# A two-layer trunk on one core: the state-space mixer's drive in two row tiles, its table fetched once, and u and y sent from other queues

## The chip, the cores and the metric

One core of a Trainium2 chip runs the whole program in one launch. The metric is device time in microseconds (us), less is better. The engines are TensorE (PE, with its weight loads shown apart as PEld), VectorE (DVE), ScalarE (ACT), GpSimd (POOL) and SyncE (SP); each takes its instructions in the order of its own queue. SP, ACT and POOL can issue DMAs; the profile shows them as SPq, ACTq and POOLq.

## The reference

The input is 256 tokens by 2048 features in float32, the depth two. Each layer is a mixer and then a gated feed-forward network with a causal convolution, both with a residual add. Layer 0 has a spatial-gating mixer; layer 1, which the change concerns, has a state-space mixer:

```python
u = h @ w_in                                     # 128 groups of 16 channels
bu = einsum('gpc,btgc->btgp', bbar, u)           # complex, 64 states per group
h_t = abar * h_{t-1} + bu_t                      # a complex diagonal recurrence over tokens
y = einsum('gcp,btgp->btgc', c_re, h.re) - einsum('gcp,btgp->btgc', c_im, h.im) + d * u
ga, gb = split(gelu(y) @ w_glu)
out = ga * sigmoid(gb)
```

## The kernel before

All large products are made on TensorE in 32-bit pieces. A weight tile (up to 1 MB, `tag="raw"`, three buffers) is fetched by SP (L108), split into units of 128x1024: ACT rounds a unit to `wh` (L124), DVE subtracts to get the rest `wl` (L125); five buffers of each. Each product then takes three matmuls, `wh` by X, `wl` by X and `wh` by X's rest (L786 and L787 in one layout, L893 to L895 in the other).

Layer 0 and its feed-forward network fill the time to about 1046 us. Then the state-space mixer follows. Its input product runs in 8 groups of two weight tiles (`form_a`, accumulators `acc`); each group gives u for two blocks of 128 features (s = 0 to 15 in all). A block s of u is then worked on in steps that the class `S5Tokens` holds, and a program of slots (one slot for each weight tile, `N_OF`, `at`, `step`) says which step of which block is traced after which tile. With n the slot of `drive`:

- `send` (L543): u goes from the tile `u` (two buffers) to DRAM (`ud`), right behind the group that made it.
- `load` (slot n-1): u comes back from DRAM in another layout, two DMAs (L551), as block-diagonal `ubd` (four buffers, off-diagonal zeros), and the matrix `pw` (L556). `load1`: the table of cosines and sines `tab` (three buffers) comes twice, to partitions 0 to 63 and again to 64 to 127 (L566). `load2` (slot n+1): `qw` and `tw` (L574, L576).
- `drive` (slot n): four matmuls of 128 rows by 128 columns of weights, `pw` by `ubd`, into the PSUM tile `ps_x` (L584).
- `take`, `scan` (n+1), `turn` (n+2): ACT copies and negates halves of `ps_x` (L597, L598), DVE multiplies by the table and adds (L599 to L609), runs the recurrence (L610) and multiplies by the table again (L623 to L625).
- `outputs` (n+3): matmuls from `ubd` with `tw` and from `sp` with `qw`, each into one half of the partitions (L639, L645).
- `gelu` (n+4): ACT makes `y`; two DMAs take it to DRAM (`yd`, L655). `fetch` (n+4): POOL brings it back as `yt` (L661). `finish` (n+6): ACT and DVE split `yt` into the operand `Gt` (L1168, L1169).

The second product (`w_glu`, tiles of `group_b` with accumulators `accb`) begins behind the eighth group, first over the blocks s = 0 to 7, and the last slots run beside it. SP's queue holds, in one order, the weights, u out and in, `pw`, `tab`, `qw`, `tw` and y; POOL's holds only `fetch`. The order of each engine's queue isn't the order of the source: the framework lays it out beforehand from simulated times and from the data dependences, and puts in the waits.

PSUM has 8 banks: three accumulators of two banks each (`acc_ps`), and two banks (`misc_ps`) that `ps_x`, `ps_y` and all small tiles share.

Of the kernel before, what the change touches and what calls it, by code (L numbers as in the profile page):

```python
# [9 lines left out]
F32 = mybir.dt.float32  # L10
# [3 lines left out]
ALU = mybir.AluOpType  # L14
PSUM = bass.MemoryType.PSUM
DRAM = bass.MemoryType.DRAM

P = 128
# [13 lines left out]
def dram(ap, offset, dims):  # L32
    return bass.AP(ap.tensor, ap.offset + offset, dims)
# [20 lines left out]
def rsqrt_column(nc, v, y, t, w):  # L54

    V = nc.vector
    V.tensor_scalar(y.bitcast(I32), v.bitcast(I32), -0.5, RSQ, ALU.mult, ALU.add)
    V.tensor_scalar(w, v, -0.5, None, ALU.mult)
    for _ in range(3):
        V.scalar_tensor_tensor(t, y, w, y, ALU.mult, ALU.mult)  # L60
        V.scalar_tensor_tensor(y, t, 1.5, y, ALU.add, ALU.mult)
# [13 lines left out]
class Weights:  # L75


    def __init__(self, nc, pool, tiles):
        self.nc, self.pool, self.tiles = nc, pool, tiles
        self.raw, self.halves = {}, {}  # L80
        self.n_dma = self.n_split = self.n_get = 0
        self.units = []
        for i, (segs, nk, width) in enumerate(tiles):
            for o in range(0, nk * width, 1024):
                self.units.append((i, o, min(1024, nk * width - o)))
        self.first_unit = {}
        for u, (i, o, n) in enumerate(self.units):
            self.first_unit.setdefault(i, u)
# [428 lines left out]
class S5Tokens:  # L517


    def __init__(self, tc, pool, psum, scr, rho, emit):  # L520
        self.nc, self.pool, self.psum = tc.nc, pool, psum
        self.scr, self.rho, self.emit = scr, rho, emit
        self.u, self.st = {}, {}
        self.ubd, self.sp = [], []
        for i in range(4):
            t = pool.tile([P, 4, P], F32, name=f"ubd{i}", tag=f"ubd{i}")
            self.nc.gpsimd.memset(t, 0.0)
            self.ubd.append(t)
        for i in range(2):
            t = pool.tile([P, 8, 64], F32, name=f"sp{i}", tag=f"sp{i}")  # L530
            self.nc.gpsimd.memset(t, 0.0)
            self.sp.append(t)
        self.rt = pool.tile([P, 8, 64], F32, name="rt")
        self.nc.gpsimd.memset(self.rt, 0.0)
# [5 lines left out]
    def send(self, s):  # L540

        ud = self.scr[4]
        self.nc.sync.dma_start(dram(ud, s * 32768, [[256, P], [1, 256]]), self.u.pop(s).rearrange("p j k -> p (j k)"))  # L543

    def load(self, s):

        nc, pool = self.nc, self.pool
        pd, qd, td, rd, ud, yd = self.scr
        ubd = self.ubd[s % 4]
        for h2 in range(2):  # L550
            nc.sync.dma_start(  # L551
                ubd[64 * h2 : 64 * h2 + 64, :, 64 * h2 : 64 * h2 + 64],
                dram(ud, s * 32768 + h2 * 4096, [[64, 64], [8192, 4], [1, 64]]),
            )
        pw = pool.tile([P, 4, P], F32, name=f"pw{s}", tag="pw", bufs=2)
        nc.sync.dma_start(pw, dram(pd, s * 65536, [[128, P], [16384, 4], [1, 128]]))  # L556
        self.st[s] = dict(pw=pw, ubd=ubd)

    def load1(self, s):

        rd = self.scr[3]
        tab = self.pool.tile([P, 2, 512], F32, name=f"tab{s}", tag="tab", bufs=3)
        lh = 8 * s % 64
        o = ((lh // 16) * P + 64 * (s // 8)) * 2048 + (lh % 16) * 64
        for i in range(2):
            self.nc.sync.dma_start(tab[64 * i : 64 * i + 64], dram(rd, o, [[2048, 64], [1024, 2], [1, 512]]))  # L566
        self.st[s]["tab"] = tab

    def load2(self, s):
# [9 lines left out]
    def drive(self, s):  # L579

        st = self.st[s]
        st["x"] = self.psum.tile([P, 512], F32, name=f"ps_x{s}", tag="misc")
        for i in range(4):
            self.nc.tensor.matmul(  # L584
                st["x"][:, i * P : (i + 1) * P], st["pw"][:, i, :], st["ubd"][:, i, :], start=True, stop=True
            )

    def take(self, s):

        nc, pool = self.nc, self.pool  # L590
        V, A = nc.vector, nc.scalar
        st = self.st[s]
        ps = st["x"]
        q = pool.tile([P, 512], F32, name=f"q{s}", tag="q", bufs=2)
        x = pool.tile([P, 512], F32, name=f"x{s}", tag="x", bufs=2)
        cos, sin = st["tab"][:, 0, :], st["tab"][:, 1, :]
        A.copy(x[0:64], ps[64:128])  # L597
        A.mul(x[64:128], ps[0:64], -1.0)  # L598
        V.tensor_tensor(q, ps, cos, op=ALU.mult)  # L599
        V.tensor_tensor(x, x, sin, op=ALU.mult)  # L600
        st["q"], st["dx"] = q, x

# [47 lines left out]
    def gelu(self, s):  # L650
        st = self.st.pop(s)
        y = self.pool.tile([P, 4, 64], F32, name=f"y{s}", tag="y", bufs=2)
        self.nc.scalar.activation(y.rearrange("q h k -> q (h k)"), st["y"][:, :256], AF.Gelu_apprx_tanh)
        for i in range(2):
            self.nc.sync.dma_start(  # L655
                dram(self.scr[5], s * 32768 + i * 16384, [[64, 64], [4096, 4], [1, 64]]), y[64 * i : 64 * i + 64]
            )

# [10 lines left out]
def tile_hybrid_trunk(  # L669
# [6 lines left out]
    nc = tc.nc  # L676
    V, A, T, G = nc.vector, nc.scalar, nc.tensor, nc.gpsimd
# [2 lines left out]
    const = ctx.enter_context(tc.tile_pool(name="const", bufs=1))  # L680
    dpool = ctx.enter_context(tc.tile_pool(name="scratch", bufs=1, space=DRAM))
    wpool = ctx.enter_context(tc.tile_pool(name="weights", bufs=1))
    acc_ps = ctx.enter_context(tc.tile_pool(name="acc_ps", bufs=3, space=PSUM))
    misc_ps = ctx.enter_context(tc.tile_pool(name="misc_ps", bufs=2, space=PSUM))


    def ffn_groups(l):
# [52 lines left out]
    rho = const.tile([P, NH], F32, name="rho")  # L740
# [6 lines left out]
    scr = []  # L747
# [86 lines left out]
    def square_sum(tp, src, dst):  # L834
        tag, bufs = tmp[0]
        junk = tp.tile([P, 512], F32, name="junk", tag=tag, bufs=bufs)
        return A.activation(junk[:, : src.shape[-1]], src, AF.Square, accum_out=dst)
# [170 lines left out]
    with ExitStack() as sgu_ctx:  # L1008
        sp = sgu_ctx.enter_context(tc.tile_pool(name="sgu", bufs=1))
# [69 lines left out]
        for g in range(4):  # L1079
            st = {}  # L1080
# [77 lines left out]


    tmp[0] = ("t", 1)  # L1160
    with tc.tile_pool(name="s5", bufs=1) as sp:

        Ys = [None] * KC

# [4 lines left out]
            V.tensor_tensor(lo, yv, hi.bitcast(F32), op=ALU.subtract)  # L1169
            Ys[s] = g  # L1170

        s5 = S5Tokens(tc, sp, misc_ps, scr, rho, emit)
        rbv = rbc.rearrange("p (k j) -> p j k", j=4)
        sched = {}

# [87 lines left out]


    tmp[0] = ("a", 2)
    with tc.tile_pool(name="ffn1", bufs=1) as fpool:
        fg = fpool.tile([P, D], F32, name="fg")
        nc.gpsimd.dma_start(fg, dram(final_g, 0, [[0, P], [1, D]]))
        oss = fpool.tile([P, 2, 4], F32, name="oss")
        tails = [[fpool.tile([P, 1], F32, name=f"o{n}{a}") for n in "svrtw"] for a in range(2)]  # L1270
        os_ = out2.rearrange("(a p) d -> p a d", p=P)

        def fin(g, pss, toks):
            cs = slice(512 * g, 512 * g + 512)
            for a in toks:
                V.tensor_tensor(hn[:, a, cs], hn[:, a, cs], pss[a], op=ALU.add)
            for a in toks:
                square_sum(fpool, hn[:, a, cs], oss[:, a, g : g + 1])
                if g < 3:
                    V.tensor_tensor(hn[:, a, cs], hn[:, a, cs], fg[:, cs], op=ALU.mult)  # L1280
                s, v, r, t, w = tails[a]
                if g == 2:
                    V.tensor_tensor(s, oss[:, a, 0:1], oss[:, a, 1:2], op=ALU.add)
                    V.tensor_tensor(s, s, oss[:, a, 2:3], op=ALU.add)
                    V.tensor_scalar(s, s, 1.0 / D, EPS, ALU.mult, ALU.add)
                if g == 3:
                    V.scalar_tensor_tensor(v, oss[:, a, 3:4], 1.0 / D, s, ALU.mult, ALU.add)
                    rsqrt_column(nc, v, r, t, w)
                    for q in range(4):
                        hq = hn[:, a, 512 * q : 512 * q + 512]  # L1290
                        if q == 3:
                            V.scalar_tensor_tensor(hq, hq, r, fg[:, cs], ALU.mult, ALU.mult)
                        elif q:
                            A.mul(hq, hq, r)
                        else:
                            V.tensor_scalar(hq, hq, r, None, ALU.mult)
                        nc.sync.dma_start(os_[:, a, 512 * q : 512 * q + 512], hq)

        ffn(1, None, fin)
# [32 lines left out]
```

## Time and profile before

| | |
|---|---|
| median of 3 runs | 2120.24 us (2118.4 to 2120.79) |
| the profiled execution | 2121.23 us, its span 2119.5 us |
| PE busy | 2090.7 us, 99% of the span |
| DVE, ACT, POOL busy | 68%, 54%, 4% |
| moved by DMA | 438.59 MB, 207 GB/s in the mean |

The span is the time from the first to the last instruction in one profiled execution; some 1.7 us of the execution lie outside it. A busy PE means that matmuls are in flight. "PEclk" is the granted share of TensorE's clock: 1 is 2.4 GHz, a half is 1.2 GHz.

### The profile page before, as it was taken

The page shows a single profiled execution, that of the slowest core. Times are in us where ns is not written, and L with a number is a line of the kernel's source. Part 1 is how long each engine was busy: PE and PEld are TensorE (multiplying, and loading weights), DVE is VectorE, ACT ScalarE, POOL GpSimd, SP SyncE. Part 2 cuts the span into 40 slices and gives each one's busy share as a digit, 9 for nine tenths or more (in the row PEclk, how much of TensorE's full clock was granted, in tenths as well). Part 3 has the DMA queues.
Part 4 walks back from the last instruction along what each step waited for, and adds up shares of the span by engine and source line. Part 5 has one row for each costly group of instructions (what it writes and reads, how often), then busy time and mean ns, then how long its engine had stood idle before and what let it go on. Part 6 is the DMA issues. An engine that isn't in the chain of part 4 may idle for free.

```text
span 2119.5 us, 27328 instructions
## 1 busy us (share of the span) xinstructions
PE 2090.7 (99%) x10279; PEld 1736.8 (82%) x10279; DVE 1439.0 (68%) x2123; ACT 1134.6 (54%) x1656; POOL 90.3 (4%) x142
## 2 busy tenths in 40 slices
PE   9999999999999999999998999999999999999998
PEld 7888888888888788888887788888888888888886
DVE  5476777886896645888788766766555656546665
ACT  6544456554555544555556556655544555445553
POOL 1010000000111110000000000000000000000000
PEclk9999999999999999999999999999999999999999
DMA  8655556666777666565799986565556555565553
GB/s 279 201 180 179 187 192 199 212 236 225 217 241 238 214 213 191 184 223 202 233 263 260 273 269 206 179 211 185 172 194 201 188 182 187 190 197 181 193 183 120
DMA packets 358597, 438.59 MB, mean 207 GB/s; under 512 B 31712, under 2 KB 275520, under 8 KB 357824
## 3 DMA queue, kind: packets, MB, share of 16 engines
q1 hardware_dynamic: 349008, 407.94, 60.5%
q0 software_dynamic: 9424, 28.88, 4.6%
q8 instruction: 81, 1.33, 0.3%
q14 instruction: 52, 0.43, 0.1%
q10 hardware_dynamic: 32, 0.01, 0.0%
HBM read 414.66 MB, written 22.02 MB: 206 GB/s over the span
## 4 chain that ended last, share of the span: by engine, by line
PE 95%; DMA 3%; DVE 1%; ACT 0%; SPq 0%; issue 0%; ACTq 0%; DVEq 0%; POOLq 0%
PE accb L893 26%; PE accb L894 26%; PE accb L895 26%; PE acc L786 4%; PE acc L787 2%; PE zt L916 2%; PE accv L987 1%; PE accv L988 1%; PE accv L989 1%; DMA w<-in_b_w_glu_dram 1%; PE pt L821 1%; DMA w<-in_b_w_in_dram 1%; DMA tab<-rd 1%; DMA ubd<-ud 0%; PE ps_x L584 0%; DMA ud<-u 0%
## 5 line engine op out<-in xcount | busy, mean ns | idle before, releaser
L125 DVE TENSOR_TENSOR wl<-w,wh 128x1024 fp32r<-128x1024 f32 (+1 forms) x721 | 879.4, 1222 | 581.2 <-ACT wh L124 577.9
L124 ACT CAST wh<-w 128x1024 fp32r<-128x1024 f32 (+1 forms) x721 | 754.1, 1050 | 744.5 <-PE accb L895 608.5
L895 PE MATMUL accb<-wh,X 128*128 128x512 f32 x1408 | 552.8, 393 | 0.0
L893 PE MATMUL accb<-wh,X 128*128 128x512 f32 x1408 | 552.1, 392 | 0.0
L894 PE MATMUL accb<-wl,X 128*128 128x512 f32 x1408 | 549.5, 390 | 0.0
L893 PE MATMUL accb<-wh,Gt 128*128 128x512 f32 x1060 | 415.8, 392 | 0.0
L895 PE MATMUL accb<-wh,Gt 128*128 128x512 f32 x1060 | 414.3, 391 | 0.0
L894 PE MATMUL accb<-wl,Gt 128*128 128x512 f32 x1060 | 414.2, 391 | 0.0
L895 PEld LDWEIGHTS accb<-wh,X 128*128 128x128 f32 x1408 | 264.4, 188 | 56.8
L894 PEld LDWEIGHTS accb<-wl,X 128*128 128x128 f32 x1408 | 264.6, 188 | 54.5
L893 PEld LDWEIGHTS accb<-wh,X 128*128 128x128 f32 x1408 | 264.5, 188 | 53.7
L893 PEld LDWEIGHTS accb<-wh,Gt 128*128 128x128 f32 x1060 | 199.2, 188 | 41.6
L895 PEld LDWEIGHTS accb<-wh,Gt 128*128 128x128 f32 x1060 | 199.2, 188 | 41.5 <-issue 0.2
L894 PEld LDWEIGHTS accb<-wl,Gt 128*128 128x128 f32 x1060 | 199.3, 188 | 41.1 <-issue 0.2
L786 PE MATMUL acc<-X,wh 128*128 128x512 f32 x512 | 184.0, 402 | 0.0
L787 PE MATMUL acc<-X,wl 128*128 128x256 f32 x512 | 144.8, 283 | 0.0
L786 PEld LDWEIGHTS acc<-X,wh 128*128 128x128 f32 x512 | 97.2, 190 | 21.8
L924 ACT ACTIVATE a<-zt,conv 128x256 f32<-128x256 f32 x176 | 94.2, 557 | 14.3 <-PE zt L916 8.2
L787 PEld LDWEIGHTS acc<-X,wl 128*128 128x128 f32 x512 | 97.9, 191 | 0.2
L943 ACT ACTIVATE z<-accb,rtok 128x512 f32<-128x512 f32 x88 | 55.7, 684 | 66.5 <-PE accb L895 66.5
L925 DVE SCALAR_TENSOR_TENSOR a<-zt,conv,a 128x255 f32<-128x255 f32 x176 | 77.7, 476 | 13.0 <-ACT a L924 13.0
L928 DVE SCALAR_TENSOR_TENSOR a<-zt,conv,a 128x254 f32<-128x254 f32 x176 | 77.1, 474 | 0.7
(299 smaller groups left out, 1407.3 us busy)
## 6 DMA issues: line engine op xcount, KB each, us to landing
w<-in_f_w_up_dram SPq DMA_DIRECT2D x352, 512.0 KB, 4.6
w<-in_f_w_down_dram SPq DMA_DIRECT2D x80, 1024.0 KB, 5.2
w<-in_b_w_glu_dram SPq DMA_DIRECT2D x64, 512.0 KB, 5.1
w<-in_a_w_in_dram SPq DMA_DIRECT2D x28, 1024.0 KB, 5.3
w<-in_a_w_out_dram SPq DMA_DIRECT2D x16, 1024.0 KB, 5.1
w<-in_b_w_in_dram SPq DMA_DIRECT2D x16, 1024.0 KB, 7.9
w<-in_f_w_down_dram SPq DMA_DIRECT2D x16, 512.0 KB, 3.7
tab<-rd SPq DMA_DIRECT2D x32, 256.0 KB, 6.7
```

The costliest lines, as they stand in the source:

```text
L124: self.nc.scalar.copy(hi[:, a:b], raw[:, o + a : o + b])
L125: self.nc.vector.tensor_tensor(lo[:, a:b], raw[:, o + a : o + b], hi[:, a:b].bitcast(F32), op=ALU.subtract)
L786: T.matmul(ps, wh, Xt[k], start=k == k_first, stop=False, skip_group_check=True)
L787: T.matmul(ps[:, NT:], wl, Xt[k][:, :NT], start=False, stop=k == ktot - 1, skip_group_check=True)
L893: T.matmul(ps[:, tt, :], xh, wh, start=k == k_first, stop=False)
L894: T.matmul(ps[:, tt, :], xh, wl, start=False, stop=False)
L895: T.matmul(ps[:, tt, :], xl, wh, start=False, stop=k == ktot - 1)
L916: T.transpose(pt[:, v * NT + tt * P : v * NT + (tt + 1) * P], z[:, tt, v * NT + q * P : v * NT + (q + 1) * P], ident,)
L924: A.activation(a[:, v], zt, AF.Identity, bias=cw[:, 3, cv : cv + 1], scale=cw[:, 2, cv : cv + 1])
L925: V.scalar_tensor_tensor(a[:, v, 1:], zt[:, : NT - 1], cw[:, 1, cv : cv + 1], a[:, v, 1:], ALU.mult, ALU.add)
L928: V.scalar_tensor_tensor(a[:, v, 2:], zt[:, : NT - 2], cw[:, 0, cv : cv + 1], a[:, v, 2:], ALU.mult, ALU.add)
L943: A.mul(z[:, tt], ps[:, tt], rtok[:, tt : tt + 1])
```

## The change

`drive` makes eight matmuls with 64 rows and 64 columns of moving data each, where it made four with 128 and 128. Since `ubd` is block-diagonal, the two halves of the rows give different columns, and each half goes to a row tile of its own (`tile_position`) and a PSUM bank of its own. `ps_x` has two banks for that and a pool of its own with one buffer; within the mixer the accumulators have two buffers, not three, and the pools of accumulators are closed and opened again before and behind it. `take` reads `ps_x` in the new order. The table is fetched once, to partitions 0 to 63, and ACT copies it to the others. `send` and the two `ubd` loads are issued by POOL, the two DMAs of y by ACT.

```diff
-        self.nc.sync.dma_start(dram(ud, ...), self.u.pop(s)...)
+        self.nc.gpsimd.dma_start(dram(ud, ...), self.u.pop(s)...)
...
         for h2 in range(2):
-            nc.sync.dma_start(
+            nc.gpsimd.dma_start(
                 ubd[64 * h2 : 64 * h2 + 64, :, 64 * h2 : 64 * h2 + 64],
...
-        for i in range(2):
-            self.nc.sync.dma_start(tab[64 * i : 64 * i + 64], dram(rd, o, [[2048, 64], [1024, 2], [1, 512]]))
+        self.nc.sync.dma_start(tab[:64], dram(rd, o, [[2048, 64], [1024, 2], [1, 512]]))
+        self.nc.scalar.copy(tab[64:], tab[:64])
...
-        st["x"] = self.psum.tile([P, 512], F32, name=f"ps_x{s}", tag="misc")
+        xt = self.xps.tile([P, 2, 512], F32, name=f"ps_x{s}", tag="x")[:, :, :256]
         for i in range(4):
-            self.nc.tensor.matmul(
-                st["x"][:, i * P : (i + 1) * P], st["pw"][:, i, :], st["ubd"][:, i, :], start=True, stop=True
-            )
+            for b in range(2):
+                o = 64 * b
+                self.nc.tensor.matmul(
+                    xt[:, b, i * 64 : i * 64 + 64], st["pw"][o : o + 64, i, :], st["ubd"][o : o + 64, i, o : o + 64],
+                    start=True, stop=True, tile_position=(o, 0),
+                )
+        st["x"] = xt.rearrange("p b (i k) -> p i b k", k=64)
...
-        A.copy(x[0:64], ps[64:128])
-        A.mul(x[64:128], ps[0:64], -1.0)
-        V.tensor_tensor(q, ps, cos, op=ALU.mult)
+        x4, q4, c4 = (t.rearrange("p (i b k) -> p i b k", i=4, b=2) for t in (x, q, cos))
+        A.copy(x4[0:64], ps[64:128])
+        A.mul(x4[64:128], ps[0:64], -1.0)
+        V.tensor_tensor(q4, ps, c4, op=ALU.mult)
...
-            self.nc.sync.dma_start(
+            self.nc.scalar.dma_start(
                 dram(self.scr[5], s * 32768 + i * 16384, [[64, 64], [4096, 4], [1, 64]]), y[64 * i : 64 * i + 64]
...
+    acc_ctx.close()
+    with ExitStack() as s5_ctx:
+        acc_ps = s5_ctx.enter_context(tc.tile_pool(name="acc_s5", bufs=2, space=PSUM))
+        xps = s5_ctx.enter_context(tc.tile_pool(name="x_ps", bufs=1, space=PSUM))
...
+        acc_ps = ffn_ctx.enter_context(tc.tile_pool(name="acc_f1", bufs=3, space=PSUM))
```

## Rows read from the trace of the kernel before

**Rows 1.** Page, part 1: PE's busy time, share, instructions
```profile
PE 2090.7 (99%) x10279; PEld 1736.8 (82%) x10279; DVE 1439.0 (68%) x2123; ACT 1134.6 (54%) x1656; POOL 90.3 (4%) x142
```
**Rows 2.** Waits of PE, 1050 to 1330 us: total, times, longest
```profile
PE ps_x L584 <- DMA ubd<-ud: 12.9, 4, 7.2
PE ps_x L584 <- DVE q L609: 1.1, 1, 1.1
```
**Rows 3.** Timeline of PE: start us, us, [idle before <-releaser]
```profile
1131.13 2.04 PE L584 MATMUL ps_x<-ubd,pw 128*128 128x128 f32 x8 [7.20 <-DMA ubd<-ud]
...
1139.51 0.66 PE L639 MATMUL ps_y<-ubd,tw 128*64 128x128 f32 x8
...
1140.81 1.13 PE L584 MATMUL ps_x<-ubd,pw 128*128 128x128 f32 x8 [0.17 <-DMA tab<-rd]
...
1147.52 0.66 PE L639 MATMUL ps_y<-ubd,tw 128*64 128x128 f32 x8
...
1186.52 2.05 PE L584 MATMUL ps_x<-ubd,pw 128*128 128x128 f32 x8 [3.37 <-DMA ubd<-ud]
```
**Rows 4.** Chain that ended last, 1100 to 1260 us: start us, us, what
```profile
1193.81 0.59 PE ps_y L639 x8
...
1212.41 0.89 PE ps_x L584 x8
1218.75 0.59 PE ps_y L639 x8
1219.34 0.47 PE ps_y L645 x16
```
**Rows 5.** Busy time of each engine by stretch; last PEclk, DMA share, GB/s
```profile
1125.00:1150.00 25.00, 17.64 (x131) 15.42 (x132) 20.16 (x29) 13.16 (x20) 1.07 (x2) 0.86 1.00 251
...
1075.00:1200.00 125.00, 110.46 (x794) 93.69 (x794) 105.48 (x138) 76.31 (x112) 6.25 (x11) 0.95 0.99 262
1059.00:1200.00 141.00, 126.46 (x888) 107.88 (x887) 114.98 (x148) 84.43 (x122) 6.25 (x11) 0.95 0.99 264
```
**Rows 6.** Timeline of SP: the two loads of ubd for s = 6
```profile
1119.23 1.25 SPq L551 DMA_DIRECT2D ubd<-ud  x2
```
**Rows 7.** DMA landing times: of ubd<-ud (by SP), then of yt<-yd (by POOL)
```profile
DMA to landing us min/median/max: 2.3/5.5/11.3
...
DMA to landing us min/median/max: 2.6/5.2/6.4
```
**Rows 8.** DMA issues, 1040 to 1330 us: count, KB each, median us to landing
```profile
q1 hardware_dynamic: 81525, 70.27, 86.2%
...
tab<-rd SPq DMA_DIRECT2D x32, 256.0 KB, 6.7
...
ubd<-ud SPq DMA_DIRECT2D x32, 64.0 KB, 5.5
yd<-y SPq DMA_DIRECT2D x32, 64.0 KB, 6.5
```
**Rows 9.** Issue durations by line: ns min/median/max, first and last start us
```profile
L655 SPq DMA_DIRECT2D yd<-y x32: 581/608/1771, 1101.7 to 1266.2; - x32
...
L661 POOL DMA_DIRECT2D yt<-yd x16: 536/537/556, 1108.6 to 1270.7; - x16
...
L471 POOL DMA_DIRECT2D td<-tt x16: 1491/1498/1557, 641.4 to 846.1; - x16
```
**Rows 10.** Groups of ACT, 1059 to 1200 us: busy, mean ns, idle before
```profile
L124 ACT CAST wh<-w 128x1024 fp32r<-128x1024 f32 x35 | 36.8, 1050 | 39.0 <-PE acc L786 21.2 <-DMA w<-in_b_w_glu_dram 11.1 <-DMA w<-in_b_w_in_dram 6.5
```
**Rows 11.** Weight loads of two lines: ns min/median/max
```profile
L584 PEld LDWEIGHTS ps_x<-ubd,pw x128: 185/192/334, 1078.2 to 1239.0; 128*128 128x128 f32 x128
...
L645 PEld LDWEIGHTS ps_y<-sp,qw x256: 132/138/139, 1097.0 to 1257.8; 128*64 128x64 f32 x128
```
**Rows 12.** Timeline of DVE: the last residual ahead of the mixer
```profile
1046.20 1.23 DVE L860 TENSOR_TENSOR hn<-accb,hn 128x1024 f32<-128x1024 f32 x1 [0.35 <-PE accb L895]
```

More of the change, by code (lines that the diff above doesn't have):

```diff
@@ L517, with __init__ @@
 class S5Tokens:
-    def __init__(self, tc, pool, psum, scr, rho, emit):
-        self.nc, self.pool, self.psum = tc.nc, pool, psum
+    def __init__(self, tc, pool, psum, xps, scr, rho, emit):
+        self.nc, self.pool, self.psum, self.xps = tc.nc, pool, psum, xps
         self.scr, self.rho, self.emit = scr, rho, emit
@@ L542, in send @@
         ud = self.scr[4]
-        self.nc.sync.dma_start(dram(ud, s * 32768, [[256, P], [1, 256]]), self.u.pop(s).rearrange("p j k -> p (j k)"))
+        self.nc.gpsimd.dma_start(dram(ud, s * 32768, [[256, P], [1, 256]]), self.u.pop(s).rearrange("p j k -> p (j k)"))
     def load(self, s):
@@ L682, in tile_hybrid_trunk @@
     wpool = ctx.enter_context(tc.tile_pool(name="weights", bufs=1))
-    acc_ps = ctx.enter_context(tc.tile_pool(name="acc_ps", bufs=3, space=PSUM))
     misc_ps = ctx.enter_context(tc.tile_pool(name="misc_ps", bufs=2, space=PSUM))
+    acc_ctx = ExitStack()
+    acc_ps = acc_ctx.enter_context(tc.tile_pool(name="acc_ps", bufs=3, space=PSUM))
     def ffn_groups(l):
@@ L1160, in tile_hybrid_trunk @@
     tmp[0] = ("t", 1)
-    with tc.tile_pool(name="s5", bufs=1) as sp:
+    acc_ctx.close()
+    with ExitStack() as s5_ctx:
+        acc_ps = s5_ctx.enter_context(tc.tile_pool(name="acc_s5", bufs=2, space=PSUM))
+        xps = s5_ctx.enter_context(tc.tile_pool(name="x_ps", bufs=1, space=PSUM))
+        sp = s5_ctx.enter_context(tc.tile_pool(name="s5", bufs=1))
         Ys = [None] * KC
@@ L1170, in emit @@
             Ys[s] = g
-        s5 = S5Tokens(tc, sp, misc_ps, scr, rho, emit)
+        s5 = S5Tokens(tc, sp, misc_ps, xps, scr, rho, emit)
         rbv = rbc.rearrange("p (k j) -> p j k", j=4)
@@ L1265, in tile_hybrid_trunk @@
     tmp[0] = ("a", 2)
-    with tc.tile_pool(name="ffn1", bufs=1) as fpool:
+    with ExitStack() as ffn_ctx:
+        acc_ps = ffn_ctx.enter_context(tc.tile_pool(name="acc_f1", bufs=3, space=PSUM))
+        fpool = ffn_ctx.enter_context(tc.tile_pool(name="ffn1", bufs=1))
         fg = fpool.tile([P, D], F32, name="fg")
```

## The prediction

> **What bounds the kernel now.** I read the page's busy times first: PE is busy for 2090.7 us [rows 1], so hardly anything but PE's own work counts, and the first question is where PE isn't busy. The waits of PE answer that: in the mixer it waits 14.5 us, of which 12.9 us, in four pieces, for `ubd<-ud` [rows 2]. The 1.1 us put down to DVE are the drive of s = 8, whose `ubd` landed just then, so I count them to the same cause. The timeline of PE shows the two long ones, 7.20 us ahead of the drive of s = 6 and 3.37 us ahead of s = 11 [rows 3]; 2.3 us stand at the first two drives. Behind a long wait the granted clock is lower: it is 0.86 in the mean from 1125 to 1150 us [rows 5], so part of that stretch ran at 1.2 GHz and the rest at 2.4. What that costs can be read from one drive with the 32 matmuls behind it: 8.38 us (1131.13 to 1139.51) against 6.71 us (1140.81 to 1147.52) [rows 3], so 1.7 us; in the same way 7.29 us (1186.52 to 1193.81) against 6.34 us (1212.41 to 1218.75) [rows 3, 4], 0.9 us. Some 17 us in all could be got back by a perfect supply.
>
> The table by stretches then says what stands next. From 1075 to 1200 us DVE is busy for 105.5 of 125 us, ACT for 76.3, and the DMA engines always (share 0.99) [rows 5]. So the cause of the waits is supply under load, but DVE is close behind PE. Whoever gives PE its `ubd` sooner gets at most what DVE leaves idle: 4.8 us from 1125 to 1150 us, where PE lost 9 [rows 5].
>
> **u's loads move to POOL: the gain.** For s = 6, SP issued the two loads at 1119.23 us [rows 6], PE asked for them at 1123.9 and got them at 1131.1 [rows 3]. So some 11 us went in landing, on a queue that moves 70.27 MB from 1040 to 1330 us [rows 8]. Landing takes 2.3 to 11.3 us on SP's queue, median 5.5; `yt`, which POOL issues in the same stage, takes 2.6 to 6.4, median 5.2 [rows 7]. The median is the same and the long tail is missing. I take this as queueing behind weights, tables and matrices in SP's queue, which a transfer on POOL's queue is spared. Then the load of s = 6 is there before PE asks at 1123.9, and so is that of s = 11, issued late too.
>
> The sum of this gain: at s = 6, 7.2 + 1.7 = 8.9 us vanish from PE, but DVE allows 4.8; at s = 11, 3.4 + 0.9 = 4.3, where DVE has room; at s = 8, 1.1. The first drive is a plain chain (u out, u in, matmul) on either queue, and I leave it. Together 10.2 us; bounds 0 (landing stays as it was) and 17.
>
> A page bears on this. The Trainium skill, "DMA: Bandwidth & Descriptors", section "Issuing engines are not separate DMA queues", says that DMAs from SP, ACT and POOL run on the same 16 engines and interleave, and that spreading them saves only the sequencer's time to issue. By it the landings would stay, and the kernel with them; the tail in the landing rows speaks against it, the equal medians for it. It is the second rival below.
>
> **What POOL has to wait for: a loss.** POOL's queue is in order, and `fetch` waits in it until y has landed. In the slots of s = 7 to 10 a load stands in the same slot as a fetch. The chain then is: outputs, up to 4 us until ACT makes gelu, 1.2 us for the two issues [rows 9], 5 to 6.5 us for `yd` [rows 8], 0.5 us for the fetch, 1.1 us for the two loads' issue if they are like the fetch and 3.0 if like `td` [rows 9], 5.2 us landing [rows 7]: 17 to 20 us. PE needs them two slots after those outputs, which at 8 us a slot (1139.51 to 1147.52) [rows 3] is 16 us. So 1 to 4 us may be missing for one or two of the four drives. I take 3 us in all; bounds 0 (the loads are laid out ahead of the fetches) and 12 (3 us at each).
>
> **SP's relief.** 16 + 32 + 32 issues go to other queues and 16 of the table fall away; at some 0.6 us each [rows 9] that is 58 us of SP in a stage of 200. ACT waited 17.6 us for weights [rows 10], but it had its rounded units ready ahead of PE and PE never waited for them, so I count nothing; at most it is part of the 17 us. The table's 16 x 256 KB = 4.2 MB less are 6% of the queue's 70.27 MB [rows 8]: it works through the landings, counted above.
>
> **ACT: a small loss.** Each block gives ACT a copy of 64x1024, at the cast's price for the same row length 1.05 us [rows 10], and two issues of 0.6 us [rows 9] behind its own gelu, say 0.2 us more: 2.45 us. Twelve blocks fall into 1059 to 1200 us: 29 us on top of 84.4 of 141 [rows 5]. That fits into 56 us of idle time, of which 21.2 was waiting for PE to free buffers [rows 10], but ACT's rounding and copies come later and DVE waits for them. 1 us; bounds 0 and what the third rival says. Half of the table is now there a copy later, but its DMA needs no second issue; even.
>
> **Drive in row tiles: nothing.** A drive takes 0.89 us for 8 passes (two for each float32 matmul), 0.111 each [rows 4]. The new one has 16 passes with half as many columns of data. What doesn't shrink is the weight load: 192 ns for 128 columns and 138 ns for 64 [rows 11] make 54 ns per 64 columns, so 108 ns for 128, the pace of the drive now. The 16 passes of the outputs take 0.47 us [rows 4], which only two column tiles side by side can (16 x 54 = 0.86). If the row tiles also load side by side, 8 x 108 = 0.87 us: no change. If the loads hide, 0.45 us, and 16 x 0.44 = 7 us less; if they go one by one, 1.73 us, and 16 x 0.84 = 13 us more. I take 0, from the slope of the load rows. The skill's "TensorEngine Tiling (Array Packing)", section "Theoretical Speedup", promises up to 2x for 64 rows, the 0.45; its "TensorE: Matmul & The Clock Gate", section "LDWEIGHTS (loading the stationary operand)", has a load's time go by columns and not by rows, which the load rows agree with and which gives the 0.87.
>
> **PSUM: a small loss.** The new accumulators begin in banks of the old ones. The 52 accumulators used up to there go round three buffers, so the last group's was the first buffer, which the mixer's first group gets again. Its first matmul, now right behind the last one of the group before, then waits until DVE has read that group's sums: 0.35 us until DVE begins and 1.23 us for its pass [rows 12], some 1.5 us (0 if another buffer is given). Two accumulators are enough within the mixer: such a pass takes 1.23 us, and a group of 64 matmuls some 11.6 (two times 1141.7 to 1147.5) [rows 3]. `ps_x` with one buffer waits for the `take` of the block before, as it did with two shared ones; nothing.
>
> **Sum.** -10.2 + 3 + 1 + 0 + 1.5 = -4.7 us. From the profiled 2121.2 (span 2119.5 and 1.7 around it) that is 2116.5; the median of the runs is 1.0 lower, so about 2115.5.
>
> **The rivals.** First, more: POOL's loads come ahead of its fetches, so nothing is lost there, DVE runs its backlog off behind 1200 us, where it has room, and the drives get shorter. -17 to -20 us and the 2.5 us of losses: 2103 to 2109. For it: SP was the only queue. Against: DVE's 105.5 of 125 us.
>
> Second, no change: the DMA engines are busy either way (0.99 [rows 5]), u still has to go out and come back, and POOL's fetches take SP's place as what `ubd` waits behind. The gain is 3 to 4 us and the losses eat it: 2116 to 2124.
>
> Third, slower, by ACT alone: the copy of the table stands in ACT's queue where the table was expected and waits there for its landing, in the median 6.7 us after issue [rows 8]. A hold of 2.7 us at each of the nine blocks from s = 2 to 10 is 24 us; with the 29 us ACT then needs 138 of 141 us and becomes the bound that the stage can't go under, and being in order it hands each hold on to DVE. The stage then grows by 5 to 10 us: 2125 to 2130. It decides from about 2 us a block; for it speaks that ACT holds for landings already (17.6 us for weights), against it that the table is issued more than a slot ahead and by an emptier SP.
>
> Fourth, slower by the weight loads one by one: +13 us less the -4.7: about 2128.
>
> **Chances.** The forecast (2109 to 2116) 0.40, first rival 0.12, second 0.24, third 0.15, fourth 0.09. I predict 2115 us. A measurement of this kernel tells about 0.2% (4.2 us) from no change. Faster by more 0.52, within 0.24, slower 0.24. Range: from 2104, into the first rival, to 2126, into the third; 0.07 lie below and 0.13 above.
>
> **What would show it.** PE's waits for `ubd` down from 12.9 to some 3 us, none of 7; `ubd` landing within 7 us; the drive at 0.85 to 0.95 us in the chain; a gap of 1.5 us at 1046; ACT at about 113 us of the same stage; DVE above 88% of it. Wrong it would be if POOL's queue is held longer by y than I reckon, if ACT waits for `tab` in long pieces, or if the drive is far from 0.89 us.

## The result, and the profile after

The changed kernel takes 2144.06 us (2143.18 to 2146.76) where the kernel before takes 2120.0 in the runs beside it: ratio 1.0117, 95% interval 1.0099 to 1.0134, so about 25 us slower. I had forecast 2115 and a range up to 2126. The profiled execution has a span of 2141.3 us, 21.8 more than before. In the profile after, the lines of `S5Tokens` stand two to five lower: the drive is L586, `take` L602 to L605, the outputs L644 and L650, gelu L658, `Gt` L1178 and L1179, the table's copy L566.

First the page's busy times, beside [rows 1]:

```profile
PE 2104.3 (98%) x10407; PEld 1742.1 (81%) x10407; DVE 1439.7 (67%) x2123; ACT 1150.8 (54%) x1672; POOL 119.2 (6%) x190
```

PE is busy for 13.6 us more and the span grows by 21.8. Next the waits of PE in the mixer, 1050 to 1330 us, beside [rows 2] (total, times, longest):

```profile
PE ps_x L586 <- DVE q L604: 7.6, 5, 2.8
PE ps_y L650 <- DVE sp L630: 5.6, 1, 5.6
PE accb L900 <- DVE wl L125: 3.2, 3, 2.2
PE accb L899 <- ACT wh L124: 2.3, 2, 1.3
PE accb L899 <- DVE z L1219: 0.9, 1, 0.9
PE accb L899 <- ACT kept L1239: 0.4, 1, 0.4
```

The 12.9 us for `ubd` are gone altogether. In their place stand 20.0 us of waiting for DVE and ACT. The table by stretches, with the first line of it beside the last of [rows 5] (PE, PEld, DVE, ACT, POOL; then granted clock, DMA share, GB/s):

```profile
1059.00:1200.00 141.00, 132.38 (x996) 110.89 (x996) 113.38 (x148) 95.00 (x135) 32.52 (x55) 0.95 0.87 245
1200.00:1300.00 100.00, 88.56 (x490) 70.03 (x489) 60.51 (x69) 55.74 (x80) 6.29 (x11) 0.93 0.65 192
```

DVE, the nearest to its limit before, is busy for 113.4 of 141 us (115.0 before), ACT for 95.0, and the DMA engines have fallen from 0.99 to 0.87. None of them is full, so the engines wait for each other. From 1200 to 1300 us PE had no idle time in the kernel before:

```profile
1200.00:1300.00 100.00, 100.00 (x552) 82.53 (x551) 68.14 (x80) 61.54 (x89) 3.76 (x7) 1.00 0.87 259
```

Now it loses 11.4 us there, and the granted clock is 0.93, so part of the stretch ran at 1.2 GHz.

How they wait can be followed at one drive, that of s = 7. The timeline of PE, then of ACT, then of DVE (start, us, what, in brackets the idle time before and what ended it):

```profile
1135.08 0.66 PE L644 MATMUL ps_y<-ubd,tw 128*64 128x128 f32 x8
1135.56 0.64 PE L650 MATMUL ps_y<-sp,qw 128*64 128x64 f32 x16
1139.00 2.54 PE L586 MATMUL ps_x<-ubd,pw 64*128 64x64 f32 x16 [2.80 <-DVE q L604]
```
```profile
1134.48 0.66 ACT L1178 CAST Gt<-yt 128x256 fp32r<-128x256 f32 x1 [0.32 <-DMA yt<-yd]
1134.55 0.58 ACTq L660 DMA_DIRECT2D yd<-y  x1
1135.98 1.04 ACT L566 COPY tab<-tab 64x1024 f32<-64x1024 f32 x1 [0.83 <-DMA tab<-rd]
...
1137.04 0.58 ACT L602 COPY x<-ps_x 64x512 f32<-64x512 f32 x1
1137.63 0.59 ACT L603 ACTIVATE x<-ps_x 64x512 f32<-64x512 f32 x1
```
```profile
1138.25 0.69 DVE L604 TENSOR_TENSOR q<-ps_x,tab 128x512 f32<-128x512 f32 x1 [1.17 <-ACT x L603]
```

Read it backwards. PE can't make the drive into the one `ps_x` until DVE has read the block before; DVE reads it when ACT's second copy from it has ended (1137.63 + 0.59, and DVE begins at 1138.25); and ACT, in order, has first to make `Gt`, for which it waits 0.32 us until `yt` lands, and the table's copy, for which it waits 0.83 until the table does. The drive stands right behind both kinds of outputs, so nothing is left for PE to do meanwhile. Behind these 2.80 idle us it runs at the lower clock: it takes 2.54 us where it takes 1.11 elsewhere, and the granted clock from 1139 to 1142 us is 0.54 in the mean. By the Trainium skill, "PSUM — Partial Sum Buffer", section "PSUM bank collisions raise a hardware error", two engines must not touch the same partitions of one bank at once, two readers included, and the compiler's scheduler puts a dependency between them. The order of these two rows agrees; the collision itself no run here shows.

The place behind the outputs isn't new. In the kernel before five drives stand so (s = 3 and 5 to 8), as many as in the changed kernel (s = 7 to 11); the drive at 1140.81 us in [rows 3], that of s = 7, is one of them. What is new is when ACT comes to `ps_x`. The first two rows are of the kernel before, the outputs ahead of that drive and ACT's first copy behind it; the other three are of the changed kernel, at the drive of s = 8:

```profile
1140.00 0.64 PE L645 MATMUL ps_y<-sp,qw 128*64 128x64 f32 x16
...
1143.39 0.58 ACT L597 COPY x<-ps_x 64x512 f32<-64x512 f32 x1
```
```profile
1150.38 1.11 PE L586 MATMUL ps_x<-ubd,pw 64*128 64x64 f32 x16
...
1156.32 1.05 ACT L566 COPY tab<-tab 64x1024 f32<-64x1024 f32 x1 [2.85 <-DMA tab<-rd]
1157.38 0.58 ACT L602 COPY x<-ps_x 64x512 f32<-64x512 f32 x1
```

From the drive's end to ACT's first copy it is 1.5 us there (1143.39 - 1141.94) and 5.9 us here (1157.38 - 1151.49). Over the five drives of each it is 0.0 to 3.2 us before and 1.3 to 10.1 us now. ACT waits 59.0 us in all for y and the table from 1050 to 1330 us (the rows are shown with a_mm4 below); in the kernel before it waited 18.1 us for y, and the table wasn't in its queue.

### The profile page after: what moved, and what is told of

Read it like the earlier page. It is cut to its first block, busy times and chain, and to the rows that moved or that the text cites. A ratio compares the mean times of both kernels' runs of the same rounds, so it can differ in the third digit from the quotient of the medians.

```text
span 2141.3 us, 27539 instructions
## 1 busy us (share of the span) xinstructions
PE 2104.3 (98%) x10407; PEld 1742.1 (81%) x10407; DVE 1439.7 (67%) x2123; ACT 1150.8 (54%) x1672; POOL 119.2 (6%) x190
## 4 chain that ended last, share of the span: by engine, by line
PE 89%; DMA 5%; DVE 2%; ACT 2%; issue 1%; ACTq 0%; SPq 0%; POOLq 0%; DVEq 0%
PE accb L899 25%; PE accb L900 25%; PE accb L901 25%; PE acc L792 4%; PE acc L793 2%; PE zt L922 2%; PE accv L993 1%; PE accv L995 1%; PE accv L994 1%; DMA yd<-y 1%; DMA yt<-yd 1%; ACT wh L124 1%; DMA tab<-rd 1%; PE pt L827 1%; DMA qd<-qt 1%
## 5 line engine op out<-in xcount | busy, mean ns | idle before, releaser
L124 ACT CAST wh<-w 128x1024 fp32r<-128x1024 f32 (+1 forms) x721 | 753.6, 1050 | 712.0 <-PE accb L901 612.3
```

Source lines behind the costliest of these rows:

```text
L124: self.nc.scalar.copy(hi[:, a:b], raw[:, o + a : o + b])
```

## The experiments

I asked first which of the parts costs, on both sides: take a part out of the changed kernel, or put it alone into the one before. Labels with a_ start from the changed kernel, those with b_ from the kernel before, and all others from a_y_sp, the changed kernel with y on SP. My theory was y's way: ACT waits at `Gt` for 40.0 us in the changed kernel, y's next issue stands behind it, and y's round trip gets longer by that.

**a_y_sp, a_u_sp, b_u_pool, b_y_act.** y back on SP, u back on SP; u alone on POOL, y alone on ACT.

```diff
 # a_y_sp: gelu of the changed kernel (b_y_act: the other way, in the one before)
-            self.nc.scalar.dma_start(
+            self.nc.sync.dma_start(
 # a_u_sp: send and load of the changed kernel (b_u_pool: the other way, in the one before)
-        self.nc.gpsimd.dma_start(dram(ud, ...
+        self.nc.sync.dma_start(dram(ud, ...
...
-            nc.gpsimd.dma_start(
+            nc.sync.dma_start(
```

> The changed kernel with y's two DMAs issued by SP again, all else as changed. Theory (y behind ACT: ACT stands in order at Gt until yt has landed, y's next issue is queued behind it, and the round trip of y thus grows): the loss goes, 2110 to 2122 us, ACT's wait at Gt from 40.0 us back to 18 to 22, PE's 5.6 us wait for sp gone. Rival a (the table's copy on ACT holds it): the 19.0 us of waits for tab stay and the loss with them, 2138 to 2146. Rival b (POOL's queue, u's loads ahead of y's fetches): 2138 to 2146. Rival c (row tiles, one buffer of ps_x, two accumulators): 2138 to 2146.

> The changed kernel with u's way out and in issued by SP again, all else as changed. Theory (y behind ACT): the loss stays and PE's waits for ubd come back, 2140 to 2155 us. Rival a (table's copy) and rival c (row tiles, PSUM): the same 2140 to 2155. Rival b (POOL's queue, u's loads ahead of y's fetches): the loss goes, 2115 to 2125, with waits for ubd of some 10 us.

> The kernel before with only u's way out and in issued by POOL. Theory (y behind ACT) and rivals a and c: no loss from this part; the 12.9 us of waits for ubd go, 2108 to 2117 us, or 2117 to 2122 if what stands behind them (DVE) takes their place. Rival b (POOL's queue): 2135 to 2145, Gt waiting for yt as in the changed kernel.

> The kernel before with only y's two DMAs issued by ACT. Theory (y behind ACT): most of the loss from this part alone, 2135 to 2150 us, ACT's wait at Gt from 18.1 to over 30 us and all of it behind 1190 us. Rivals a, b and c: 2118 to 2124, Gt's wait as before.

Measured: a_y_sp 2134.24 us, ratio 1.0066 (1.0049 to 1.0083); a_u_sp 2145.36, 1.0118 (1.0103 to 1.0133); b_u_pool 2115.34, 0.9971 (0.9959 to 0.9982); b_y_act 2121.77, 1.0009 (0.9999 to 1.0019). My theory had to give back the whole loss in the first run and show it in the last. It gave back 10 of 24 us, and y alone costs nothing that can be told. It falls as the cause of the whole. POOL's queue falls too: u on POOL is a gain by itself. One thing in a_u_sp went against what I expected: with u on SP again the waits for `ubd` don't come back (PE waits 0.2 us for it, `ubd` lands within 8.8 us), and the time is that of the changed kernel, 1.0118 against 1.0117. So beside the new drive u on POOL gains nothing that can be told. What b_u_pool shows in PE's waits, 1050 to 1330 us, beside [rows 2]:

```profile
PE ps_x L584 <- DMA pw<-pd: 1.9, 1, 1.9
PE ps_y L645 <- DMA qw<-qd: 1.5, 2, 1.0
PE ps_y L639 <- DMA tw<-td: 1.4, 1, 1.4
PE ps_x L584 <- DMA ubd<-ud: 0.7, 1, 0.7
```

`ubd` has gone from 12.9 to 0.7 us, and 4.8 us for the matrices, which stay on SP, are new. PE's queue is another one too: a single drive (s = 3) stands right behind both kinds of outputs in it, where five did.

**a_tab2, a_y_sp_tab2, b_u_tab, b_dma_tab.** The table fetched twice again; the copy put into the kernel before with u on POOL, and with both moves.

```diff
 # a_tab2; a_y_sp_tab2 has y on SP besides (b_u_tab, b_dma_tab: the other way, on b_u_pool and with y on ACT)
-        self.nc.sync.dma_start(tab[:64], dram(rd, o, [[2048, 64], [1024, 2], [1, 512]]))
-        self.nc.scalar.copy(tab[64:], tab[:64])
+        for i in range(2):
+            self.nc.sync.dma_start(tab[64 * i : 64 * i + 64], dram(rd, o, [[2048, 64], [1024, 2], [1, 512]]))
```

> The changed kernel with the table fetched twice by SP again and no copy on ACT, all else as changed. Theory now (the table's copy on ACT: ACT, in order, stands at it until the table has landed, 19.0 us in twelve pieces in the changed kernel and 32.2 with y on SP, and everything behind it in ACT's queue, y's issues too, gets later): most of the loss goes, 2118 to 2127 us. Rival c (row tiles, one buffer of ps_x, two accumulators): 2135 to 2145. Both a share: 2127 to 2135.

> The changed kernel with y's DMAs on SP and the table fetched twice: what is left of the change is the row tiles with their PSUM, and u on POOL. Theory (table's copy): 2114 to 2121 us, near the kernel before with u on POOL alone (2115.3), more by the 1.3 us at the mixer's start and some 3 to 5 us of longer drives. Rival c (row tiles, PSUM): 2129 to 2136, as with the copy.

> The kernel before with u's way on POOL and the table fetched once and copied by ACT; no row tiles, PSUM as before, y on SP. Theory (table's copy): slower than u on POOL alone (2115.3) by 8 to 15 us, 2123 to 2131. Rival c (row tiles, PSUM): 2113 to 2118, no cost of the copy.

> The changed kernel without its row tiles and its PSUM pools: the kernel before with u on POOL, y on ACT and the table copied by ACT. Theory (table's copy, made worse by y's issues behind it): 2130 to 2142 us. Rival c (row tiles, PSUM): 2114 to 2120. If copy and y on ACT cost only their own holds (no more than the sum of each alone): 2124 to 2131.

Measured: 2136.43 us, 1.0078 (1.0057 to 1.0099); 2136.53, 1.0077 (1.0062 to 1.0092); 2109.68, 0.9950 (0.9935 to 0.9965); 2117.36, 0.9986 (0.9977 to 0.9995). The table's copy isn't the cause: without it 16 of the 24 us stay, with y on SP nothing goes with it (2136.5 against 2134.2), and put into the kernel before it is a gain. b_u_tab is the fastest kernel so far. What all slow ones have in common is the new drive with its PSUM.

**mm4, mm4_misc, rt_x2.** From a_y_sp: the old drive and the old `take`, with `ps_x` in its own pool with one buffer (mm4) or shared as before (mm4_misc); or the new drive with two places for `ps_x`.

```diff
 # mm4 (mm4_misc: self.psum and tag "misc")
-        xt = self.xps.tile([P, 2, 512], F32, name=f"ps_x{s}", tag="x")[:, :, :256]
+        st["x"] = self.xps.tile([P, 512], F32, name=f"ps_x{s}", tag="x")
         for i in range(4):
-            for b in range(2):
...
+            self.nc.tensor.matmul(
+                st["x"][:, i * P : (i + 1) * P], st["pw"][:, i, :], st["ubd"][:, i, :], start=True, stop=True
+            )
 # rt_x2, one tile self.xt for all blocks
+        xt = self.xt[:, :, 256 * (s % 2) : 256 * (s % 2) + 256]
```

> The changed kernel with y on SP (2134.2 us), and with the drive and the take of before: four matmuls of 128 rows into one bank. ps_x keeps its own pool with one buffer, the accumulators have two buffers in the mixer, the table is copied by ACT, u goes by POOL. Against it stands the same without any change of the drive or of PSUM: 2109.7. If the row tiles are the cause (their longer drive, and what is laid out behind it): 2108 to 2115. If the PSUM pools are (one ps_x, two accumulators, pools closed and opened again): 2128 to 2136.

> As the run with four matmuls, but ps_x shares the two buffers of ps_y as before; only the accumulators differ from the kernel before in PSUM, two in the mixer where it had three, with pools closed and opened again. If the one buffer of ps_x is the cause: 2108 to 2114. If the two accumulators are: 2125 to 2136. If the row tiles are: 2108 to 2114 here too, and the run with four matmuls and one ps_x as well.

> The changed kernel with y on SP (2134.2 us), and with two places for ps_x: the same two banks, held once, block after block in the left and in the right half of each. Row tiles and two accumulators stay. If the one buffer of ps_x is the cause: 2110 to 2122, PE's wait for q at the drive (8.8 us) gone. If the two accumulators or the row tiles themselves are: 2130 to 2138.

Measured: 2116.71 us, 0.9978 (0.9969 to 0.9987); 2111.16, 0.9948 (0.9932 to 0.9964); 2134.08, 1.0056 (1.0034 to 1.0079). So the drive it is: 17.5 us between a_y_sp and mm4, which differ in the drive, in the place of its `ps_x` and the order in which `take` reads it, and in nothing else. Two accumulators cost nothing that can be told (0.9948 against 0.9950); one buffer of `ps_x` costs 0.3%, 6 us. rt_x2 says nothing on the buffer: PE still waits for `q` at the drive, 9.0 us in six pieces.

**mm8, rt_seq, rt_load, rt_out.** Is it the row tiles in the hardware? A drive is only some 0.3 us longer. But ahead of the chip the framework lays out every queue from the instructions it is given, and with eight matmuls it lays them out otherwise. mm8 has eight matmuls on all 128 rows: the instructions of each of the five engines stand in the same order as in a_y_sp, line for line, in the records of the two traces.

```diff
 # mm8, from a_y_sp
-                    xt[:, b, i * 64 : i * 64 + 64], st["pw"][o : o + 64, i, :], st["ubd"][o : o + 64, i, o : o + 64],
-                    start=True, stop=True, tile_position=(o, 0),
+                    xt[:, b, i * 64 : i * 64 + 64], st["pw"][:, i, :], st["ubd"][:, i, o : o + 64],
+                    start=True, stop=True,
 # rt_seq, from a_y_sp
-        for i in range(4):
-            for b in range(2):
+        for b in range(2):
+            for i in range(4):
 # rt_load, from a_y_sp: the steps of a slot; rt_out: ..., s5.scan, s5.drive, s5.load2, s5.load, s5.load1, s5.outputs
-            s5.gelu, s5.take, s5.finish, s5.fetch, s5.turn, s5.scan, s5.outputs, s5.drive, s5.load2, s5.load, s5.load1
+            s5.load, s5.load1, s5.load2, s5.gelu, s5.take, s5.finish, s5.fetch, s5.turn, s5.scan, s5.outputs, s5.drive
```

> The changed kernel with y on SP (2134.2 us, drives of 16 passes at some 0.34 us more than the old drive with what follows it), and with its eight matmuls on all 128 rows, so without row tiles: two banks, the new order of ps_x, and the order of every queue laid out as with row tiles. If the row tiles themselves cost (some slow mode of the engine): faster, 2118 to 2130. If they save weight loading, side by side: the drive goes to about 16 x 0.108 = 1.7 us, some 10 us more, 2139 to 2148. If neither: 2134.

> The changed kernel with y on SP (2134.2 us), the row tiles not in turn: four matmuls in the upper 64 rows, then four in the lower. The layout of the queues stays but for two places. If the two row tiles work side by side only when they alternate: drives of some 1.7 us and 2140 to 2147. If one matmul hides the next one's load in either order: the drive at 1.0 to 1.1 us, 2132 to 2137.

> The changed kernel with y on SP (2134.2 us), its drive untouched; only the order in the source of a slot's steps is another: the loads are named first, not last. By that drive and outputs no longer stand at one place in PE's queue. If two thirds of the row tiles' cost is the order that the queues got (waits of PE for take, wl and wh, and the half clock behind them, 11 of 17 us), the time must move by many us though no operation differs: 2115 to 2128. If the cost sits in the drive itself: 2132 to 2136.

> As the run with the loads named first, another order again: the outputs are named last in a slot, behind drive and loads. If the order of the queues is what costs: a time that differs from 2134.2 by more than 4 us, in either direction, 2115 to 2150. If the drive itself costs: 2132 to 2136.

In rt_load and rt_out the load of a block stands ahead of the outputs of the block four earlier, which has the same `ubd`: those outputs are made from another block's u, with the same amount of work.

Measured: mm8 2134.88 us, 1.0063 (1.0041 to 1.0085); rt_seq 2137.56, 1.0072 (1.0054 to 1.0089); rt_load 2127.91, 1.0031 (1.0019 to 1.0043); rt_out 2131.64, 1.0042 (1.0026 to 1.0059). One undisturbed drive of each from the timeline of PE: a_y_sp, rt_seq, mm8, and mm4 with the old drive:

```profile
1212.73 1.11 PE L586 MATMUL ps_x<-ubd,pw 64*128 64x64 f32 x16
```
```profile
1213.79 1.60 PE L586 MATMUL ps_x<-ubd,pw 64*128 64x64 f32 x16
```
```profile
1214.60 1.89 PE L586 MATMUL ps_x<-ubd,pw 128*128 128x64 f32 x16
```
```profile
1217.52 1.05 PE L584 MATMUL ps_x<-ubd,pw 128*128 128x128 f32 x8
```

mm8's drives are 0.78 us longer by these rows, 12.5 us over sixteen. PE's next matmul begins 0.58 us later behind them, 9.3 us over sixteen. The time is still that of a_y_sp, 2134.9 against 2134.2; by the two intervals they could lie some 6 us apart. So within this order of the queues the drive's length does not set the time; what it takes away from waiting it gives to work (PE's waits from 1050 to 1330 us are 11.4 us in mm8 and 15.8 in a_y_sp, and the granted clock from 1059 to 1200 us is 0.99 and 0.95, from there to 1300 us 0.98 and 1.00). rt_seq's drives, 0.49 us longer, move nothing clear either (1.0072 against 1.0066). And with the drive untouched another order gives 6.3 us back (rt_load, where one drive stands right behind both kinds of outputs, and not five). That run counts for less, since its outputs wait for other loads. rt_out also has one such drive, and its 2.6 us lie within the scatter of both.

**b_mm8, a_mm4, b_dma.** The last three: eight plain matmuls in the kernel before with u on POOL and the table copied, into the one bank of before; the whole change but for the drive; both DMA moves alone.

```diff
 # b_mm8, from b_u_tab
         for i in range(4):
-            self.nc.tensor.matmul(
-                st["x"][:, i * P : (i + 1) * P], st["pw"][:, i, :], st["ubd"][:, i, :], start=True, stop=True
-            )
+            for b in range(2):
+                o = 64 * b
+                self.nc.tensor.matmul(
+                    st["x"][:, i * P + o : i * P + o + 64], st["pw"][:, i, :], st["ubd"][:, i, o : o + 64],
...
 # a_mm4: mm4 with y's two DMAs by nc.scalar; b_dma: b_u_pool with the same
```

> The kernel before with u on POOL and the table copied (2109.7 us), and its drive in eight plain matmuls of 128 rows by 64 columns into the same bank; PSUM as before, no row tiles, y on SP. The queues then get the same bunched order as in the changed kernel (outputs and the next drive at one place in PE's queue, from s = 5 on). If the order that comes with eight matmuls is the cause: 2126 to 2138. If PSUM's pools are needed for the loss: 2110 to 2122, the drives' own 0.84 us each at most.

> The whole change but for the drive: four matmuls of 128 rows into one bank, as before; y on ACT, u on POOL, the table copied, one ps_x, two accumulators. If the eight-matmul drive is the cause of the loss: 2144.1 falls to 2116.7 (the same with y on SP) and y's 7 us on ACT, 2120 to 2126. If y on ACT is a cause of its own with the other parts: 2130 to 2140.

> The kernel before with both DMA moves and nothing else: u by POOL, y by ACT. u alone gave 2115.3 and y alone 2121.8. If y on ACT costs little by itself: 2114 to 2119. If it costs the 7.7 us that it costs beside the table's copy (2117.4 against 2109.7): 2121 to 2125.

Measured: b_mm8 2136.60 us, 1.0072 (1.0052 to 1.0092); a_mm4 2115.83, 0.9980 (0.9970 to 0.9991); b_dma 2123.10, 1.0009 (1.0000 to 1.0019). Eight matmuls make the kernel slow without any of the changed PSUM; of b_mm8's 27 us over b_u_tab up to 14 may be the drives' own length (PE's next matmul begins 0.90 us later behind each). In its queue five drives stand right behind both kinds of outputs, s = 7 to 11. And the whole change without the eight is faster than the kernel before. The same views of a_mm4 show how. PE's waits, 1050 to 1330 us; then the timelines of PE and of ACT around the drives of s = 6 and 7:

```profile
PE accb L895 <- DVE wl L125: 1.5, 2, 0.8
PE ps_x L584 <- issue: 1.5, 3, 1.0
PE accb L894 <- ACT wh L124: 0.8, 1, 0.8
PE acc L787 <- DVE X L809: 0.4, 1, 0.4
PE ps_y L645 <- DVE sp L625: 0.2, 1, 0.2
```
```profile
1128.50 1.05 PE L584 MATMUL ps_x<-ubd,pw 128*128 128x128 f32 x8
...
1129.60 0.66 PE L639 MATMUL ps_y<-ubd,tw 128*64 128x128 f32 x8
...
1134.15 0.69 PE L645 MATMUL ps_y<-sp,qw 128*64 128x64 f32 x16
...
1136.87 1.13 PE L584 MATMUL ps_x<-ubd,pw 128*128 128x128 f32 x8 [1.01 <-issue]
```
```profile
1134.74 0.58 ACT L597 COPY x<-ps_x 64x512 f32<-64x512 f32 x1
1135.34 0.59 ACT L598 ACTIVATE x<-ps_x 64x512 f32<-64x512 f32 x1
...
1136.95 0.66 ACT L1173 CAST Gt<-yt 128x256 fp32r<-128x256 f32 x1
...
1138.80 1.03 ACT L566 COPY tab<-tab 64x1024 f32<-64x1024 f32 x1
```

Here the drive, the first outputs and the second stand apart, with matmuls of the product between them, and ACT takes `ps_x` ahead of `Gt` and of the table. PE is held by the same reader here too, but for less: the 1.01 us ahead of the second drive, put down to "issue", end just behind DVE's reading of the block before (1136.09 + 0.68):

```profile
1136.09 0.68 DVE L599 TENSOR_TENSOR q<-ps_x,tab 128x512 f32<-128x512 f32 x1
```

In the changed kernel five drives stand right behind both kinds of outputs, here none, and at the drive shown above ACT comes to `ps_x` last. Three views of waits from 1050 to 1330 us, of ACT in the changed kernel, of DVE there, and of ACT in a_mm4, where DVE waits for `x` nowhere:

```profile
ACT Gt L1178 <- DMA yt<-yd: 40.0, 12, 6.5
ACT tab L566 <- DMA tab<-rd: 19.0, 8, 4.2
```
```profile
DVE q L604 <- ACT x L603: 17.0, 11, 3.8
```
```profile
ACT Gt L1173 <- DMA yt<-yd: 24.4, 9, 5.9
ACT tab L566 <- DMA tab<-rd: 11.3, 5, 4.2
```

And the table by stretches of a_mm4, beside that of the changed kernel:

```profile
1059.00:1200.00 141.00, 138.77 (x968) 114.87 (x968) 124.53 (x162) 106.38 (x150) 35.65 (x60) 1.00 1.00 275
1200.00:1300.00 100.00, 97.63 (x511) 79.47 (x510) 66.07 (x79) 61.86 (x87) 3.27 (x6) 0.98 0.68 212
```

The two spans differ by 27.0 us (2141.3 and 2114.3). PE's waits in this stretch are 20.0 and 4.4 us: 15.6. A drive with the four matmuls behind it takes 2.07 us against 1.81 and begins 0.09 later behind its forerunner: 16 x 0.35 = 5.6. The 5.8 left I put down to the half clock, which by the two clocks of the stretches is worth at most 0.05 x 141 + 0.05 x 100 = 12 us, less what of it fell on idle time.

These waits are the changed kernel's own. a_y_sp_tab2 is nearly as slow (2136.5 us) with other ones; there PE waits for these two most:

```profile
PE ps_y L650 <- DVE sp L630: 6.7, 1, 6.7
PE ps_x L586 <- DVE Gt L1179: 5.6, 1, 5.6
```

Nor does the number of drives right behind both kinds of outputs rank the runs: a_tab2 has two and takes 2136.4 us, the kernel before has five and takes 2120. What the slow builds share is the drive in eight matmuls, not one wait.

## Why the prediction failed, by its own steps

Laid one on the other, by their ratios (one thousandth is 2.1 us):

| with, besides | us | ratio | step, us |
|---|---|---|---|
| u on POOL (b_u_pool) | 2115.34 | 0.9971 | -6.1 |
| table copied (b_u_tab) | 2109.68 | 0.9950 | -4.5 |
| two accumulators (mm4_misc) | 2111.16 | 0.9948 | -0.4 |
| `ps_x` alone, one buffer (mm4) | 2116.71 | 0.9978 | +6.4 |
| y on ACT (a_mm4) | 2115.83 | 0.9980 | +0.4 |
| drive in eight matmuls (after) | 2144.06 | 1.0117 | +29.0 |

A step's size hangs on what is there already; the table is one way through them.

- **u's loads to POOL: right in the kernel before, as far as it can be told.** I had -10.2 and +3 for POOL's fetches; it is -6.1. In b_u_pool `ubd` lands within 7.8 us (7.4 in the changed kernel), and the long tail of [rows 7] is gone, as I took from the rows; the median isn't lower (6.5 us, and 5.4 in the changed kernel, against 5.5). No fetch held a load up: 0.7 us of waiting. What was missing is the 4.8 us for `pw`, `qw` and `tw`, next in line on SP. But b_u_pool has another order of the queues too, and a_u_sp has no waits for `ubd` to speak of with u on SP; how much of the -6.1 is POOL's queue isn't measured by itself.
- **The table's copy: wrong in sign, small.** I had it within +1 us of ACT; it is -4.5, and the two intervals still overlap a little. ACT had the idle time for the copy, and the 4.2 MB less, which I had counted at nothing of their own, are the likely reason: in b_u_tab PE waits for none of the three matrices for which it waits in b_u_pool. My third rival, ACT held at the copy, is there to be seen in the waits: 11.3 us in a_mm4, where it decides nothing, and 19.0 in the changed kernel, where 7.6 of the 24 us go with the copy (a_tab2).
- **y on ACT: no price of its own.** Part of the same +1. Measured: nothing that can be told in the order of the table above (+0.4), alone (1.0009), and in the changed kernel without the copy (2136.4 against 2136.5); but 7.8 us beside u on POOL (2123.1 against 2115.3), 7.7 with the copy besides (2117.4 against 2109.7), and 9.8 in the changed kernel. Each build has other queues, and the same move stands in another place in each.
- **PSUM.** The boundary: 1.5 us forecast, 1.32 found, in one row of PE's timeline of the changed kernel:

```profile
1047.84 0.66 PE L827 MATMUL pt<-ident,hn 128*128 128x128 f32 x4 [1.32 <-DVE hn L866]
```

  The row's matmul is a transpose that needs `hn` itself, so it doesn't show that a bank was what PE waited for; the wait ends with the DVE pass that I had named. Two accumulators enough: right. "`ps_x` with one buffer [...] nothing": wrong, 6.4 us. I had reasoned that two shared buffers bound the drive as one does; mm4 against mm4_misc says they didn't.
- **The drive: the step that failed.** "Drive in row tiles: nothing" was priced by passes and weight loads alone. By these it nearly held: 1.04 us in the chain and not 0.87, 16 x 0.15 to 0.35 us. (The load rows that I went by all had 128 rows; the loads of the new drive, of 64 rows and 128 columns, take 188 ns in the median against 192.) What I left out is that eight instructions in place of four give the framework another program to lay out. My own description of the kernel said that the order isn't the source's; the sum then moved parts about in the old order as if it would stay. Against the same parts with four matmuls (a_mm4), the eight leave five drives right behind both kinds of outputs, as in the kernel before, and put ACT's reading of `ps_x` behind its two waits for DMAs. The 15.6 us of waits that this adds, and the 5.8 us that I put down to the half clock, are some 21 of the 27 us between the two traces. Of the prices of the drive that I had bounds for (-7 to +13) none could reach it.
- **What would have shown it.** `ubd` waits 0 (forecast 3), landing to 7.4 (7), gap 1.32 (1.5): right. Drive 1.04 (0.85 to 0.95), ACT 95.0 us of the 141 (113), DVE 80% (over 88): wrong, and the last two in a direction that I hadn't thought of, everyone idler. In a_mm4, with the old drive, they are 106.4 us and 88%, the ubd waits 0, and its 2115.83 us is near the 2115.5 of my sum; two errors of 5 to 6 us (table, one `ps_x`) cancel in that.
- **The rivals.** More, no change, slower by ACT, and weight loads one by one: none is what happened. The fourth had the right place and the wrong price: sixteen loads one by one are what the plain eight pay, 1.73 us in b_mm8's chain as I had it, but mm8 shows that such a length costs nothing, to some 6 us, in the order of a_y_sp; in b_mm8 it may be half of the loss:

```profile
1231.09 1.73 PE ps_x L586 x16
```

What is shown: the eight-matmul drive is the cause (a_mm4 against the changed kernel, mm4 against a_y_sp, b_u_tab against b_mm8). The row tiles as such are not, since mm8 without them is as slow. The drive's length is at most 5.6 of the 27 us in the changed kernel, and the waits in the rows above are most of the rest. That the order of the queues makes these waits is the best reading of mm8 and rt_load, but it is argued: no run has the row tiles in the order of a_mm4, so the share of the order isn't measured by itself, and the place behind the outputs alone doesn't make them, since the kernel before has it too. Why the framework lays out eight matmuls so stays open.

## What to carry to other kernels

Where a framework lays out the queues, price a change twice: once by what its instructions take, and once by asking which wait now stands ahead of which reader, since a few instructions more can move both. If a change has several parts, build them up one on the other: here five were worth -4 us together, and one that looked neutral by its durations cost 29. The version to keep is that with u on POOL and the table copied, with the old drive, PSUM and y's way: 2109.68 us, 0.9950 (0.9935 to 0.9965).

## What the runs showed of the hardware

Sixteen passes on two row tiles of 64 rows took 1.11 us in turn, 1.60 us with one tile's eight ahead of the other's, and 1.89 us on all 128 rows. So the two tiles save 0.78 of 1.89 us when their matmuls alternate and 0.29 one after the other. By when PE's next matmul begins it is 0.58 and 0.08 us: side by side in turn, hardly otherwise. The Trainium skill, "TensorEngine Tiling (Array Packing)", section "Theoretical Speedup", has up to 2x for 64 rows; the trace shows 1.7x against the same matmuls without tiles, and none against half as many with 128 columns, 1.05 us.
